# Two heads' values as high and low halves of one stationary operand in a dilated attention layer

## The chip, the cores and the metric

The kernel runs on one core of one Trainium2 chip. The metric is the device time of one execution in microseconds (us); the number shown is the median over runs.

## What is computed

Two layers on 512 tokens of width 1024, in fp32. Layer 0 mixes by stick-breaking attention, layer 1 by the dilated attention that this change touches; each is followed by a feed-forward block and a gate. The dilated attention has three groups with dilation 1, 4 and 16, eight heads of width 64 in each. A group's attention is banded and gives, beside its output, the logarithm of the sum of its weights; the groups are then mixed by a softmax over these logarithms. That equals one softmax over the keys of all three groups together, which is what the kernel computes.

```python
for g, (window, dil) in enumerate(((128, 1), (512, 4), (2048, 16))):
    q = apply_partial_rope(proj[:, :, g, 0], cos, sin)
    k = apply_partial_rope(proj[:, :, g, 1], cos, sin)
    v = proj[:, :, g, 2]
    ...
    o, lse = banded_attention(strided(q), strided(k), strided(v), window // dil)
    ...
alpha = jax.nn.softmax(jnp.stack(lses, axis=0), axis=0)
o = jnp.einsum('gbsh,gbshd->bshd', alpha, jnp.stack(outs, axis=0).astype(jnp.float32)).astype(x.dtype)
return o.reshape(B, S, H * HEAD_DIM) @ w_out
```

## The kernel before

Every fp32 product is made of high and low parts in the fp32r type by three matmuls: high x high, low x high, high x low (`mm3`, L257 to L259; `linear`, L356 to L360; `value_step`, L667 to L669). Weights arrive in 220 units of 128x1024 by SP's transfers; ACT makes the high part (L98), DVE the low part (L99).

TensorE (PE) runs in program order. `Filler` puts pieces of the projections (queries, keys, values, output products) between the attention's steps by a clock that the steps advance. The order on ACT, DVE, GpSimd (POOL) and SP comes from a scheduler that simulates the program with priorities (`due`, the table `TUNE`). PSUM has two banks for projections (`bank`, shown as mmb and out) and six others (`wide`, shown as wb).

`dilated` (L640 to 945) works in this order. The values of groups 1 and 2 for the first four heads are projected into four wide banks, those of group 0 for all heads into two of each kind; `value_part` empties them, high part by ACT (L680), low part by DVE (L681), 128 columns (two heads) at a time. `sq.row` in between spreads the norm's factors over a bank with fp32 calls (L311) and DVE copies them to `rrow` (L320). Then for each of four pairs of heads: `scores` (matmuls L731, mask and maximum by DVE L741), `maxima` over the three groups (transposes L749 to L763, steps on `m` L755 to L757), and `exps`, 16 exponentials on ACT (L778). Group 0 is in natural order of the tokens (order 0); groups 1 and 2 share a second order (order 1), in which a token 4r + c stands at c x 128 + r; `cut` and `sigma` are the two views.

`attend` runs after the maxima of pairs 0 and 1 for one pair, and at the end for pairs 2 and 3 together, with the rest of the values and the first output products between (`between`; the exponentials of the last pair that are in `late` wait for the last values). A pair has eight jobs (head, order, half of the tokens). `turn` transposes a job's weights (L794), and ACT and DVE make the high and low part (`th` L800, `tl` L801). `apply` multiplies them with the values. It runs `ahead` (3) jobs behind `turn`. The stationary operand is 128 columns wide, 64 of them values and 64 ones (zeros in the low part), so that the sums of the weights come out in the other half of the bank:

```python
vs, vp = slice(64 * h, 64 * h + P), pr % 2 if g else pr
mm3(out[:, j * P:j * P + width], v[:, 0, vp, vs], v[:, 1, vp, vs],
    th[:, at:at + width], tl[:, at:at + width], j == 0 and g < 2, True)
```

After each head the two orders' banks are added (ACT L856, DVE L858); after each pair `divide` takes four reciprocals of `den` (L833), one after each following job, then the product (L835) and the split into `od` (L262, L264), with which `out` multiplies the output weights.

Of the kernel before, what the change touches and what calls it, by code (L numbers as in the profile page):

```python
# [29 lines left out]
            hps=2, blag=1.5, vlag=0.0, fx=5.5, ahead=3, pgap=0.0, vev1=50)  # L30
# [4 lines left out]
C_ID, C_NEG, C_TRI, C_M0, C_M1, C_M2, C_ROPE, C_END = 0, 128, 256, 384, 640, 768, 896, 898  # L35

# [6 lines left out]
def constants():  # L43
    i = np.arange(P)
    c = np.zeros((P, C_END), np.float32)
    c[:, C_ID:C_ID + P] = np.eye(P)
    c[:, C_NEG:C_NEG + P] = np.where(i[:, None] >= i[None, :], -BIG, 0.0)
# [116 lines left out]
def program(tc, ctx, w_dram, x_dram, xs_dram, p_dram, pos_dram, g_dram, c_dram, out_dram):  # L164
# [33 lines left out]
    nc.sync.dma_start(consts, c_dram)  # L198
# [441 lines left out]
    def dilated(xh, xl, sq, oh, ol, partial, out, prepare):  # L640
        swap = list(range(8, 16)) + list(range(8)) + list(range(16, 32))
        with tc.tile_pool(name="dlw", bufs=1, reuse_waits="tile") as wp:
            V, norm, qk, whole = {}, {}, {}, []
# [6 lines left out]
            def ones_and_zeros():  # L650

                for v in whole:
                    n = v.shape[3]
                    pool.tensor_copy(v[:, :, 0, :, 64:128], ones[:, 0:1, None, None].to_broadcast([P, 4, n, 64]))
                    pool.tensor_scalar(v[:, :, 1, :, 64:128], ones[:, 0:1, None, None].to_broadcast([P, 4, n, 64]),
                                       0.0, None, ALU.mult)
# [14 lines left out]
            def value_part(g, t, ps):  # L671
                v = V[g, t]
# [97 lines left out]
            def exps(S, N):  # L770
                done = []
                for h in range(2):
                    for order in range(2):
                        for i in range(4):
                            s = S[h, order, i // 2]
                            a, b = (i % 2) * 256 + (P if (i == 0 and order == 0) else 0), (i % 2 + 1) * 256
                            with due("exps"):
                                done.append(act.activation(s[:, a:b], s[:, a:b], AF.Exp, bias=N[:, order, i, h:h + 1],  # L778
                                                           scale=0.125))
                return done  # L780

            def turn(S, order, h, j2):
# [3 lines left out]
                for j in (2 * j2, 2 * j2 + 1):  # L786
# [10 lines left out]
                th = wp.tile([P, T], F32R, name="th", tag="th", bufs=3)  # L797
                tl = wp.tile([P, T], F32R, name="tl", tag="tl", bufs=3)
# [4 lines left out]

            def apply(pr, order, h, j2, th, tl, out):
                at = 0
                for j in (2 * j2, 2 * j2 + 1):
# [4 lines left out]
                    for g, width in jobs:  # L811
                        v = V[g, j]
                        vs, vp = slice(64 * h, 64 * h + P), pr % 2 if g else pr
                        mm3(out[:, j * P:j * P + width], v[:, 0, vp, vs], v[:, 1, vp, vs],
                            th[:, at:at + width], tl[:, at:at + width], j == 0 and g < 2, True)
                        at += width
                fill.clock += 1.3

            def attend(prs, gap, between=None):
                jobs = [(pr, order, h, j2) for pr in prs for h in range(2) for order in range(2) for j2 in range(2)]  # L820
                outs, sums = {}, {}
# [8 lines left out]
                def divide(pr, num, den):  # L830
                    for c in range(4):
                        cs = slice(c * P, (c + 1) * P)
                        i = dve.reciprocal(den[:, cs], den[:, cs])  # L833
                        if c == 3:
                            dve.tensor_mul(num, num, den)  # L835
# [26 lines left out]
                for d in list(later):  # L862
                    run(d)
# [333 lines left out]
```

## Time and profile before

| | |
|---|---|
| median of three runs | 1458.36 us (1457.98, 1461.53, 1458.36) |
| the profiled execution | 1462.61 us |
| its span | 1460.5 us, mean granted clock 0.984 |
| PE busy | 1419.4 us, 97% |
| DVE busy | 910.5 us, 62% |
| ACT busy | 639.8 us, 44% |
| the dilated attention | about 714 to 1030 us of the span |

A row of a group of instructions has line, engine, operation, what is written and read (partitions x elements, type) and how many, then busy us, mean ns of one, and idle time just before them with what ended it. A timeline's row starts with start and length. Matmuls are pipelined: their listed lengths overlap, so what one costs PE is the distance from its start to the next. An fp32 call to the matmul stands as two records.

### The profile page before, as it was taken

The numbers are of one execution on the slowest core, as the hardware profiler recorded it, in microseconds if no ns is written. First come the engines' busy times: TensorE is split into PE (matmuls) and PEld (weight loads), VectorE is DVE, ScalarE is ACT, GpSimd is POOL, SyncE is SP. The second block draws the span as 40 slices with busy tenths as digits, with TensorE's granted clock in tenths as the row PEclk, the third lists the DMA queues.
The fourth block names the chain that finished last, engine by engine and source line by source line (L and its number), as shares of the span: only waits on it lengthen the run. The fifth ranks groups of instructions, "written<-read, shape, count | busy, mean of one in ns | idle before, by whom it ended". The sixth has DMA issues, their size and how long they took to land.

```text
span 1460.5 us, 18457 instructions
## 1 busy us (share of the span) xinstructions
PE 1419.4 (97%) x7250; PEld 1194.4 (82%) x7250; DVE 910.5 (62%) x1539; ACT 639.8 (44%) x970; POOL 56.9 (4%) x33
## 2 busy tenths in 40 slices
PE   8999999999999999999989999999999999999998
PEld 7888988888888888887868878788888888888877
DVE  4788886584353544568758886956783443535476
ACT  4788985543231222345542433444732322312353
POOL 0111110000000000001200000000000000000000
PEclk9999999999999999999999998999999999999999
DMA  5344351433333333223322211220432332333321
GB/s 201 101 115 119 111 134 58 137 95 101 100 89 100 94 94 101 87 85 117 109 72 88 73 57 45 73 74 14 145 101 89 100 101 87 101 92 96 101 76 70
DMA packets 45127, 138.80 MB, mean 95 GB/s; under 512 B 5680, under 2 KB 6448, under 8 KB 45040
## 3 DMA queue, kind: packets, MB, share of 16 engines
q1 hardware_dynamic: 44960, 137.36, 31.2%
q8 instruction: 57, 0.93, 0.3%
q0 software_dynamic: 80, 0.26, 0.1%
q14 instruction: 30, 0.25, 0.0%
HBM read 123.45 MB, written 4.19 MB: 87 GB/s over the span
## 4 chain that ended last, share of the span: by engine, by line
PE 87%; DVE 8%; ACT 2%; issue 1%; DMA 1%; SPq 0%; ACTq 0%; DVEq 0%
PE wb L356 17%; PE wb L358 16%; PE wb L360 16%; PE mmb L356 5%; PE mmb L360 5%; PE mmb L358 5%; DVE wlo L99 2%; PE wb L258 1%; PE wb L259 1%; PE wb L257 1%; PE mmb L419 1%; PE mmb L421 1%; PE mmb L420 1%; PE wb L731 1%; PE z L259 1%
## 5 line engine op out<-in xcount | busy, mean ns | idle before, releaser
L98 ACT ACTIVATE whi<-wraw_t 128x1024 fp32r<-128x1024 f32 (+1 forms) x298 | 229.2, 800 | 468.3 <-PE wb L360 345.7
L99 DVE TENSOR_TENSOR wlo<-wraw_t,whi 128x1024 fp32r<-128x1024 f32 (+1 forms) x310 | 276.2, 912 | 238.8 <-ACT whi L98 233.7
L356 PE MATMUL wb<-nh,whi 128*128 128x512 f32 (+1 forms) x594 | 227.1, 385 | 4.3 <-ACT nh L262 4.3
L358 PE MATMUL wb<-nh,wlo 128*128 128x512 f32 (+1 forms) x594 | 226.1, 383 | 0.0
L360 PE MATMUL wb<-nl,whi 128*128 128x512 f32 x576 | 207.4, 390 | 0.4 <-DVE nl L266 0.4
L356 PE MATMUL wb<-fh,whi 128*128 128x512 f32 x496 | 196.2, 396 | 0.0
L358 PE MATMUL wb<-fh,wlo 128*128 128x512 f32 x496 | 196.2, 396 | 0.0
L360 PE MATMUL wb<-fl,whi 128*128 128x512 f32 x496 | 196.2, 396 | 0.0
L356 PEld LDWEIGHTS wb<-nh,whi 128*128 128x128 f32 x594 | 111.6, 188 | 28.8 <-ACT nh L262 6.9
L358 PEld LDWEIGHTS wb<-nh,wlo 128*128 128x128 f32 x594 | 111.6, 188 | 21.8
L360 PEld LDWEIGHTS wb<-nl,whi 128*128 128x128 f32 x576 | 107.7, 188 | 23.4 <-DVE nl L266 1.2
L356 PEld LDWEIGHTS wb<-fh,whi 128*128 128x128 f32 x496 | 93.2, 188 | 22.6
L360 PEld LDWEIGHTS wb<-fl,whi 128*128 128x128 f32 x496 | 93.2, 188 | 22.5
L358 PEld LDWEIGHTS wb<-fh,wlo 128*128 128x128 f32 x496 | 93.2, 188 | 22.5
L356 PE MATMUL mmb<-nh,whi 128*128 128x512 f32 x248 | 102.2, 412 | 3.6 <-DVE V L681 3.6
L360 PE MATMUL mmb<-nl,whi 128*128 128x512 f32 x248 | 98.9, 399 | 0.0
L358 PE MATMUL mmb<-nh,wlo 128*128 128x512 f32 x248 | 98.9, 399 | 0.0
L1087 DVE TENSOR_TENSOR f<-wb,f 128x512 f32<-128x512 f32 (+1 forms) x50 | 33.3, 667 | 73.6 <-PE wb L360 71.2
L1062 DVE TENSOR_TENSOR z<-wb,rrow 128x512 f32<-128x512 f32 x60 | 40.6, 688 | 55.7 <-PE wb L360 55.7
L1065 ACT ACTIVATE fh<-z 128x512 fp32r<-128x512 f32 x64 | 39.9, 632 | 77.1 <-DVE z L1063 77.0
L356 PEld LDWEIGHTS mmb<-nh,whi 128*128 128x128 f32 x248 | 48.1, 194 | 13.6 <-issue 4.0
L289 DVE TENSOR_TENSOR acc<-acc,sq 128x512 f32<-128x512 f32 (+1 forms) x74 | 48.9, 661 | 15.6 <-ACT sq L285 15.0
(817 smaller groups left out, 2665.3 us busy)
## 6 DMA issues: line engine op xcount, KB each, us to landing
wraw_t<-w SPq DMA_DIRECT2D x219, 512.0 KB, 3.6
x<-x SPq DMA_DIRECT2D x8, 256.0 KB, 6.9
h<-xs SPq DMA_DIRECT2D x8, 256.0 KB, 5.6
spill<-h SPq DMA_DIRECT2D x8, 256.0 KB, 2.7
h<-spill SPq DMA_DIRECT2D x8, 256.0 KB, 5.5
out<-h SPq DMA_DIRECT2D x7, 256.0 KB, 2.1
praw<-p SPq DMA_DIRECT2D x4, 256.0 KB, 4.0
wraw_t<-w SPq DMA_DIRECT2D x4, 128.0 KB, 3.1
```

What stands on the lines that cost most here:

```text
L98: self.highs.append(self.nc.scalar.activation(hi[:, c], src[:, c], AF.Copy))
L99: self.lows.append(self.nc.vector.tensor_sub(lo[:, c], src[:, c], hi[:, c].bitcast(F32)))
L257: pe.matmul(ps, ah, bh, start=start, stop=False, skip_group_check=True)
L258: pe.matmul(ps, ah, bl, start=False, stop=False, skip_group_check=True)
L259: pe.matmul(ps, al, bh, start=False, stop=stop, skip_group_check=True)
L289: self.adder.tensor_tensor(self.acc[:, cs], self.acc[:, cs], self.sq[:, cs], ALU.add)
L356: pe.matmul(ps[m][:, cs], wh, xh[k][:, cs], start=(k == 0 and cs is not TWO[1]), stop=False, skip_group_check=True)
L358: pe.matmul(ps[m][:, cs], wl, xh[k][:, cs], start=False, stop=False, skip_group_check=True)
L360: pe.matmul(ps[m], wh, xl[k], start=False, stop=(k == nk - 1), skip_group_check=True)
L1062: dve.tensor_mul(z, ps, norm["row"])
L1065: act.activation(a, z, AF.Copy)
L1087: dve.tensor_add(y[m][:, cs], ps, y[m][:, cs])
```

## The change

The tile of values holds for each head its high and low part side by side, so one stationary operand of 128 columns is high | low, and a job is multiplied by two matmuls (th, tl) instead of three. Its bank then has th x high + tl x high in 64 rows and th x low + tl x low in the other 64, which are added afterwards (L874 and L875 of the new file). The sums of the weights come from the exponentials' own accumulators, `D`; ACT widens them to 64 columns for each head (`wD`), and eight fp32 calls for each pair (L844, L847) spread them over a bank that the reciprocals read. Both orders go to one bank, `av`: order 0 is transposed with a permuted identity (`sorter`) and written in runs of 32 columns (`mixed`). `ahead` is 4, the buffers of th and tl are 5. `value_part` is one instruction on each engine for a bank's part.

```diff
-                v = wp.tile([P, 4, 2, 2 if g else 4, 192], F32R, name=f"V{g}")
-                whole.append(v)
+                v = wp.tile([P, 4, 4 if g else 8, 2, 64], F32R, name=f"V{g}")
...
-                for pr in range(2 if g else 4):
-                    at = (t % 2 if g else 0) * 256 + pr * P
-                    src = ps[:, at:at + P].rearrange("p (h d) -> p h d", h=2)
-                    hi, lo = (v[:, i, pr, :].rearrange("p (h d) -> p h d", h=3)[:, 0:3:2] for i in range(2))
-                    with due("vev1"):
-                        norm["last"] = act.activation(hi, src, AF.Copy, scale=c)
-                        dve.scalar_tensor_tensor(lo, src, c, hi.bitcast(F32), ALU.mult, ALU.subtract)
+                at = (t % 2 if g else 0) * 256
+                src = ps[:, at:at + (256 if g else 512)].rearrange("p (h d) -> p h d", d=64)
+                hi, lo = (V[g, t][:, :, i] for i in range(2))
+                with due("vev1"):
+                    norm["last"] = act.activation(hi, src, AF.Copy, scale=c)
+                    dve.scalar_tensor_tensor(lo, src, c, hi.bitcast(F32), ALU.mult, ALU.subtract)
...
                                 done.append(act.activation(s[:, a:b], s[:, a:b], AF.Exp, bias=N[:, order, i, h:h + 1],
-                                                           scale=0.125))
-                return done
+                                                           scale=0.125, accum_out=D[:, order, i, h:h + 1]))
+                wD = wp.tile([P, 2, 4, 2, 64], F32, name="wD")
+                with due("exps"):
+                    act.activation(wD, D[:, :, :, :, None].to_broadcast([P, 2, 4, 2, 64]), AF.Copy)
+                return done, wD
...
-                        pe.transpose(ps[:, n:n + P], part, ident)
+                        pe.transpose(ps[:, n:n + P], part, ident if order else sorter)
...
+            def mixed(ap, a, n):
+
+                return ap.rearrange("p (r c m) -> p c r m", r=4, c=4)[:, a // P:(a + n) // P]
+
...
-                        mm3(out[:, j * P:j * P + width], v[:, 0, vp, vs], v[:, 1, vp, vs],
-                            th[:, at:at + width], tl[:, at:at + width], j == 0 and g < 2, True)
+                        v = V[g, j][:, (pr % 2 if g else pr) * 2 + h].rearrange("p a d -> p (a d)")
+                        dst = out[:, j * P:(j + 1) * P] if order else mixed(out, j * P, width)
+                        for t in (th, tl):
+                            src = t[:, at:at + width]
+                            pe.matmul(dst, v, src if order else src.rearrange("p (c r m) -> p c r m", r=4, m=32),
+                                      start=(j == 0 and order == 0 and t is th), stop=(order == 1 and t is tl),
+                                      skip_group_check=True)
...
-                fill.clock += 1.3
+                fill.clock += 0.9
...
+                    ps = wide()
+                    for order in (1, 0):
+                        for i in range(4):
+                            d = DD[pr][:, order, i].rearrange("p a d -> p (a d)")
+                            if order:
+                                pe.matmul(ps[:, i * P:(i + 1) * P], d, ident, start=(i == 0), stop=False,
+                                          skip_group_check=True)
+                            else:
+                                pe.matmul(mixed(ps, i * P, P), d, sorter.rearrange("p (c r m) -> p c r m", r=4, m=32),
+                                          start=False, stop=True, skip_group_check=True)
+                    fill.clock += 1.8
                     for c in range(4):
                         cs = slice(c * P, (c + 1) * P)
-                        i = dve.reciprocal(den[:, cs], den[:, cs])
...
+                        yield dve.reciprocal(den[:, cs], ps[:, cs])
...
-                            act.activation(s1, outs[1], AF.Copy)
-                            for dst, src in ((den[hs], ds), (num[hs], hs)):
-                                dve.tensor_tensor(cut(dst), sigma(outs[0][src]), cut(s1[src]), ALU.add)
+                            act.activation(num[hs], av[ls], AF.Copy)
+                            dve.tensor_tensor(num[hs], av[hs], num[hs], ALU.add)
                         if h == 1:
-                            later.append(divide(pr, num, den))
+                            dve.tensor_mul(num, num, den)
+                            oh[pr], ol[pr] = split(num, f"od{pr}")
```

Not shown: the permuted identity is a part of the constants' input, which one more transfer of SP brings; `ones_and_zeros` (six POOL instructions that filled the ones and zeros) is gone; a pair's `divide` starts with the pair's first job, one piece after each job, and `attend` no longer runs what is left of it behind its loop.

The order on DVE, behind the copy to `natural` in the norm before the dilated layer (`V` are the low parts of values, `ang`, `turns`, `angle` and `mag` steps of the rope's angles, `wlo` a weight's low part). Before:

```order
L297 COPY natural<-acc 128x4x128
L305 TENSOR_SCALAR ms<-mmb 128x8
L99 TENSOR_TENSOR wlo<-wraw_t,whi 128x1024
L681 SCALAR_TENSOR_TENSOR V_5870<-wb,rcol,V_5870 128x2x64
L681 SCALAR_TENSOR_TENSOR V_5871<-wb,rcol,V_5871 128x2x64
L681 SCALAR_TENSOR_TENSOR V_5870<-wb,rcol,V_5870 128x2x64
L618 CAST ang<-pos_i 128x512
L681 SCALAR_TENSOR_TENSOR V_5871<-wb,rcol,V_5871 128x2x64
L681 SCALAR_TENSOR_TENSOR V_5870<-wb,rcol,V_5870 128x2x64
L681 SCALAR_TENSOR_TENSOR V_5871<-wb,rcol,V_5871 128x2x64
L619 TENSOR_SCALAR ang<-ang,consts 128x512
L681 SCALAR_TENSOR_TENSOR V_5870<-wb,rcol,V_5870 128x2x64
L320 COPY rrow<-mmb 128x512
```

and in the change, from its angle's fifth step on:

```order
L628 SCALAR_TENSOR_TENSOR angle<-turns,ang 128x512
L629 SCALAR_TENSOR_TENSOR angle<-turns,angle 128x512
L675 SCALAR_TENSOR_TENSOR V_5871<-wb,rcol,V_5871 128x4x64
L630 SCALAR_TENSOR_TENSOR angle<-turns,angle 128x512
L675 SCALAR_TENSOR_TENSOR V_5871<-wb,rcol,V_5871 128x4x64
L675 SCALAR_TENSOR_TENSOR V_5872<-wb,rcol,V_5872 128x4x64
L632 TENSOR_SCALAR angle<-angle 128x512
L675 SCALAR_TENSOR_TENSOR V_5871<-wb,rcol,V_5871 128x4x64
L322 COPY rrow<-mmb 128x512
L634 TENSOR_SCALAR mag<-angle 128x512
L101 TENSOR_TENSOR wlo<-wraw_t,whi 128x1024
```

Seven pieces of values of 128 columns and the weight's low part stood ahead of `rrow`; now four of 256 do, and the weight's low part is behind it.

The order on ACT, at the exponentials of the third pair (`kh` and `qh` are the high parts of a split, `whi` a weight's). Before:

```order
L778 ACTIVATE S<-S,negmax 128x128
L778 ACTIVATE S<-S,negmax 128x256
L98 ACTIVATE whi<-wraw_t 128x1024
L778 ACTIVATE S<-S,negmax 128x256 x8
L778 ACTIVATE S<-S,negmax 128x128
L262 ACTIVATE qh<-rf_8021 128x512
L778 ACTIVATE S<-S,negmax 128x256 x5
L98 ACTIVATE whi<-wraw_t 128x1024
L262 ACTIVATE kh<-rf_8086 128x512
```

and in the change:

```order
L774 ACTIVATE S,D<-S,negmax 128x128
L774 ACTIVATE S,D<-S,negmax 128x256 x9
L774 ACTIVATE S,D<-S,negmax 128x128
L264 ACTIVATE kh<-rf_7978 128x512
L774 ACTIVATE S,D<-S,negmax 128x256 x3
L100 ACTIVATE whi<-wraw_t 128x1024
L774 ACTIVATE S,D<-S,negmax 128x256 x2
L778 ACTIVATE wD<-D 128x1024
```

The split of k stood behind all 16 exponentials and a weight's split, and now stands behind 11 exponentials; the copy to `wD` follows the sixteenth.

The order on PE, at the start of the last attend (`S` are weights, `out` the first output products). Before:

```order
L794 MATMUL wb<-consts,S 128x128 x11
L257 MATMUL wb<-th,V_5869 128x256
L258 MATMUL wb<-tl,V_5869 128x256
L259 MATMUL wb<-th,V_5869 128x256
```

and in the change:

```order
L793 MATMUL wb<-consts,S 128x128 x15
L820 MATMUL wb<-th,V_5870 128x2x4x32
L820 MATMUL wb<-tl,V_5870 128x2x4x32
L820 MATMUL wb<-th,V_5870 128x2x4x32
L820 MATMUL wb<-tl,V_5870 128x2x4x32
L793 MATMUL wb<-consts,S 128x128 x4
L844 MATMUL wb<-consts,wD 128x128 x4
L847 MATMUL wb<-consts,wD 128x4x32 x4
L259 MATMUL out<-od0h,whi 128x512
```

Four more transposes stand ahead of the first apply, two matmuls take the place of three, and the sums' calls follow the next transposes.

## Rows read from the trace of the kernel before

**Rows 1.** The page's first part: busy us, share of the span, instructions.
```profile
PE 1419.4 (97%) x7250; PEld 1194.4 (82%) x7250; DVE 910.5 (62%) x1539; ACT 639.8 (44%) x970; POOL 56.9 (4%) x33
```

**Rows 2.** Waits of PE, 700 to 1030: us in total, times, longest.
```profile
PE mmb L667 <- DVE rrow L320: 3.8, 1, 3.8
PE mmb L356 <- DVE V L681: 3.6, 1, 3.6
PE wb L763 <- DVE m L757: 1.9, 1, 1.9
PE out L257 <- DVE V L681: 1.9, 1, 1.9
...
PE wb L731 <- ACT kh L262: 1.1, 1, 1.1
...
PE wb L731 <- DVE kl L264: 0.9, 1, 0.9
PE wb L763 <- DVE m L756: 0.7, 1, 0.7
```

**Rows 3.** Windows: length, busy us (instructions) by engine, PE clock, DMA share, GB/s.
```profile
734.00:738.00 4.00, 4.00 (x12) 3.13 (x11) 3.97 (x13) 1.35 (x5) 0.00 (x0) 0.57 0.02 4
872.00:878.00 6.00, 6.00 (x18) 4.78 (x19) 2.79 (x5) 3.82 (x10) 0.00 (x0) 0.51 0.30 87
946.00:953.00 7.00, 6.82 (x30) 5.83 (x31) 4.91 (x34) 0.63 (x1) 0.00 (x0) 0.51 0.23 77
990.00:994.00 4.00, 4.00 (x17) 3.48 (x16) 0.07 (x1) 3.90 (x10) 0.00 (x0) 0.57 0.00 0
```

**Rows 4.** Groups by form, PE, 700 to 1030: busy us, mean ns | idle before.
```profile
L259 PE MATMUL wb<-th,V 128*128 128x128 f32 x72 | 20.1, 279 | 0.0
...
L259 PE MATMUL wb<-th,V 128*128 128x256 f32 x24 | 7.0, 294 | 0.0
```

**Rows 5.** Timeline of PE in three places: start, us, engine, line, operation.
```profile
727.99 1.05 PE L311 MATMUL mmb<-consts,rcol 128*128 128x128 f32 x8
728.80 0.48 PE L667 MATMUL mmb<-whi,uh 128*128 128x512 f32 x1
...
978.81 0.28 PE L667 MATMUL mmb<-whi,nh 128*128 128x256 f32 x1
...
981.93 0.28 PE L669 MATMUL mmb<-wlo,nh 128*128 128x256 f32 x1
...
994.27 0.27 PE L259 MATMUL wb<-th,V 128*128 128x128 f32 x1
...
995.28 0.28 PE L259 MATMUL wb<-th,V 128*128 128x128 f32 x1
```

**Rows 6.** Timeline of DVE at 732.
```profile
732.85 0.69 DVE L320 COPY rrow<-mmb 128x512 f32<-128x512 f32 x1
```

**Rows 7.** Timeline of ACT and PE at 754 to 760.
```profile
754.56 0.37 ACT L680 ACTIVATE V<-mmb,rcol 128x128 fp32r<-128x128 f32 x1 [2.52 <-PE mmb L669]
...
760.19 0.47 PE L356 MATMUL mmb<-nh,whi 128*128 128x512 f32 x1 [3.63 <-DVE V L681]
```

**Rows 8.** Groups by form, DVE, 700 to 1030.
```profile
L801 DVE TENSOR_TENSOR tl<-wb,th 128x512 fp32r<-128x512 f32 x24 | 16.0, 678 | 10.6 <-ACT th L800 10.4
...
L833 DVE RECIPROCAL den<-den 128x128 f32<-128x128 f32 x16 | 13.9, 917 | 0.0
...
L741 DVE DVE_READ_ACCUMULATOR2_ANT M<- 128x1 f32 x96 | 7.9, 82 | 0.0
```

**Rows 9.** Timeline of PE, two groups of transposes four jobs apart.
```profile
997.04 0.62 PE L794 MATMUL wb<-consts,S 128*128 128x128 f32 x4
...
1002.84 0.62 PE L794 MATMUL wb<-consts,S 128*128 128x128 f32 x4
```

**Rows 10.** Timeline of PE at 55, and the answer on line 481 (two runs of 128).
```profile
54.99 0.33 PE L483 MATMUL z<-sb0qa,sb0la 128*128 128x256 f32 x1
...
L481 PE MATMUL z<-rconst x16: 328/328/332, 55.2 to 225.8; 128*128 128x256 f32 x16
```

More of the change, by code (lines that the diff above doesn't have):

```diff
@@ L29 @@
             fb=0.32, slope=0.05, lag=8.0, gap=1.2, m0=6.0, m1=5.5, m2=8.0, p0=5.0, p1=2.0, p2=8.0, hp0=6, hp1=30,
-            hps=2, blag=1.5, vlag=0.0, fx=5.5, ahead=3, pgap=0.0, vev1=50)
+            hps=2, blag=1.5, vlag=0.0, fx=5.5, ahead=4, pgap=0.0, vev1=50)
 NUNIT = 220
@@ L44, in constants @@
     i = np.arange(P)
-    c = np.zeros((P, C_END), np.float32)
+    c = np.zeros((P, C_ALL), np.float32)
     c[:, C_ID:C_ID + P] = np.eye(P)
+    c[:, C_SORT:C_SORT + P] = np.eye(P)[:, i.reshape(32, 4).T.reshape(-1)]
     c[:, C_NEG:C_NEG + P] = np.where(i[:, None] >= i[None, :], -BIG, 0.0)
@@ L771, in exps @@
                 done = []
+                D = wp.tile([P, 2, 4, 2], F32, name="D")
                 for h in range(2):
@@ L828, in attend, with divide @@
                     between()
-                def divide(pr, num, den):
+                def divide(pr, den):
+                    ps = wide()
[9 more added lines that the diff above has]
+                    fill.clock += 1.8
                     for c in range(4):
                         cs = slice(c * P, (c + 1) * P)
-                        i = dve.reciprocal(den[:, cs], den[:, cs])
-                        if c == 3:
-                            dve.tensor_mul(num, num, den)
-                            oh[pr], ol[pr] = split(num, f"od{pr}")
-                            later.clear()
-                        yield i
-                for n, (pr, order, h, j2) in enumerate(jobs):
-                    if j2 == 0:
-                        outs[order] = wide()
-                    apply(pr, order, h, j2, *ready.pop(0), outs[order])
+                        yield dve.reciprocal(den[:, cs], ps[:, cs])
+                for n, (pr, order, h, j2) in enumerate(jobs):
+                    if order == 0 and j2 == 0:
+                        if h == 0:
+                            sums[pr] = tmp("num"), tmp("den")
+                            later.append(divide(pr, sums[pr][1]))
+                        av = wide()
+                    apply(pr, order, h, j2, *ready.pop(0), av)
                     if n + ahead < len(jobs):
@@ L847, in attend @@
                     if later:
-                        after(next(later[0]), norm["turned"])
+                        i = next(later[0], None)
+                        if i is None:
+                            later.clear()
+                        else:
+                            after(i, norm["turned"])
                     if order == 1 and j2 == 1:
-                        if h == 0:
-                            sums[pr] = tmp("num"), tmp("den")
                         num, den = sums[pr]
-                        s1 = tmp("s1")
-                        hs, ds = HALF[h], HALF[1 - h]
+                        hs, ls = HALF[h], HALF[1 - h]
                         with due("comb"):
-                            act.activation(s1, outs[1], AF.Copy)
-                            for dst, src in ((den[hs], ds), (num[hs], hs)):
-                                dve.tensor_tensor(cut(dst), sigma(outs[0][src]), cut(s1[src]), ALU.add)
+                            act.activation(num[hs], av[ls], AF.Copy)
+                            dve.tensor_tensor(num[hs], av[hs], num[hs], ALU.add)
                         if h == 1:
-                            later.append(divide(pr, num, den))
+                            dve.tensor_mul(num, num, den)
+                            oh[pr], ol[pr] = split(num, f"od{pr}")
                     tick(gap)
-                for d in list(later):
-                    run(d)
             vps = {g: [wide(), wide()] for g in (1, 2)}
@@ L924, in dilated @@
                 N = maxima(MM[pr])
-                late = exps(SS[pr], N)[TUNE["late"]:]
+                late, DD[pr] = exps(SS[pr], N)
+                late = late[TUNE["late"]:]
                 fill(TUNE["m2"])
```

27 lines of the change are left out of this document (10 added, 17 removed).

## The prediction

> **What bounds the kernel now.** I read the page's busy times first. TensorE (PE) is busy for 97% of the span, VectorE (DVE) for 62%, ScalarE (ACT) for 44% [rows 1]. So a matmul that goes is worth its own time, and work on the other engines is worth only what PE waits for. Then I read the waits of PE over the dilated attention, 700 to 1030 us [rows 2]: all seven that stand there, 13.9 us together, are of kinds that the change touches. Third, the windows in which the granted clock fell: 0.51 to 0.57 in the stretches just behind those waits, the lower of the two levels for most of the stretch [rows 3]. A wait can therefore cost more than its own length, and I take the loss behind it as (1 - clock) times the stretch: 1.7 us behind 734, 2.9 behind 872, 3.4 behind 946, 1.7 behind 990.
>
> The sum is made against the profiled execution of 1462.61 us (span 1460.5). The median of the runs, 1458.36, lies 4.25 lower; I subtract the sum's gain from the median, as the runs will be.
>
> **Matmuls removed and added.** The third matmul of every product with the weights goes: 72 of 128 columns and 24 of 256 [rows 4]. What one costs is its distance to the next, not its listed duration, for they are pipelined: from 994.27 to 995.28 there are nine steps, 0.112 each; from 978.81 to 981.93 26 steps, 0.120 each [rows 5]. 72 x 0.112 + 24 x 0.120 = 10.9 us. Added are 32 fp32 calls that spread the sums (8 for each pair of heads). The kernel has such calls already, in the row that spreads a column: four calls are eight records, 727.99 to 728.80, 0.101 each [rows 5]. 64 x 0.101 = 6.5 us. Net gain 4.4 us; with the added ones at 0.112, 3.7.
>
> By the Trainium skill ("TensorE: Matmul & The Clock Gate", Back-to-back issue gap) a sustained stream of 128-column matmuls runs at about 81 ns each. Taken for both kinds, that page would make the net (96 - 64) x 0.081 = 2.6 us, an estimate; the rows here show 0.112, and I keep them.
>
> **The rrow wait, 3.8 us.** PE needs a bank that DVE empties with the copy to rrow, at 732.85 for 0.69 [rows 6]. Ahead of it in DVE's order stood a weight split, seven pieces of values and two steps of the angle. In the new order four pieces of 256 and eight steps of the angle are ahead, and the split is behind. Those pieces can go as their banks fill, and the angle's steps between them, while PE still works on the last ones; the copy's own source is written by the calls from 727.99 to 728.80 [rows 5]. So the copy should start about 729 and end about 729.8. PE asked at 732.85 + 0.69 - 3.84 = 729.7, but one late piece is 0.5, so I keep 0.7 as the wait: gain 3.1. The low clock behind it (1.7) I count half, 0.9, because a short wait stays. Bounds 0 and 5.5.
>
> **The wait for group 0's values, 3.6 us.** Values of the first group are emptied in 32 pieces of 128 that pass between ACT and DVE with weight splits in between; the first starts at 754.56, yet PE gets its bank at 760.19, 3.63 after it asked [rows 7]. Now it is one ACT and one DVE instruction of 512 for each bank. By the 512-wide th and tl of this kernel (DVE's is 678 ns [rows 8]) a bank is empty about 1.3 us after its last matmul, 754.56 + 1.3 = 755.9, before PE asks at 756.56. Gain 3.6, with 0 as the lower bound if weight splits stand between them as they did before.
>
> **The waits at the maxima, 1.9 + 0.7 us.** Pair 1's maxima wait for two DVE steps on m. Ahead of them stood four reciprocals in one go and a sum that are now elsewhere or gone: 4 x 0.87 (13.9 us for 16) and one step of 512 at tl's 0.68, 4.2 us less on DVE [rows 8], more than both waits. Gain 2.6, and half of the low clock behind them, 1.4, since other work of DVE's could still come late. Bounds 0 and 5.5.
>
> **The waits for kh and kl, 1.1 + 0.9 us.** ACT split k only after all 16 exponentials of the pair and a weight split; now it stands after 11. That is five exponentials and one split earlier, but the accumulators add to each exponential, by the nearest row up to 82 ns, DVE's read of its accumulator [rows 8]: 11 x 0.08 = 0.9 back. And DVE's kl has its own queue. I take half: 1.0, and a quarter of the low clock, 0.9. Bounds -1 and 5.4.
>
> **The wait for an out bank, 1.9 us.** It ends with the last of the second half's values, which ACT and DVE hand to and fro in 128-wide pieces. Half the instructions are left. Gain 1.9, and half of the low clock, 0.9. Bounds 0 and 3.6.
>
> **What the last attend may cost.** Here PE has nothing to fill with but a few output products. A pair is eight jobs, twice the four between 997.04 and 1002.84 [rows 9], 11.6 us. Now it takes 11.6 - (18 x 0.112 + 6 x 0.120) + 16 x 0.101 = 10.5. DVE's share of a pair: six tl of 512 columns at 0.68 and two of 384 at three quarters of it, 5.1; four reciprocals, 3.5; two adds, the product and the split of num at 0.68 each, 2.7 [rows 8]: 11.3, less where neighbours overlap. The two are about level, and the last pair's reciprocals, which stood behind the loop, are now in it. So PE may wait on tl in each pair. I charge 2.0 of waits and one low stretch of 1.6, 3.6 in all; bounds 0 and 8. Five th and tl buffers and one more turn ahead work against it: the first apply now follows 15 transposes, not 11, so its th has more time.
>
> **Covered.** The four 1024-wide copies of the sums (at most 1.4 us each, twice tl's 0.68) and the accumulators' reads (64 x 0 to 82 ns, at most 5.2 us [rows 8]) lie on ACT, 44% busy; in the last attend they delay th by up to 2 us, which is inside the bound of 8. The half-size num steps, the ones and zeros gone from GpSimd and the extra transfer of 64 KB at SP's head, next to loads that run at the start, are off PE's path. If ACT's cover were gone the accumulators would cost those 5.2.
>
> **Sum.** 4.4 + (3.1 + 0.9) + 3.6 + (2.6 + 1.4) + (1.0 + 0.9) + (1.9 + 0.9) - 3.6 = 17.1 us. Against the profiled 1462.6 that is 1445.5; against the median **1441.3**. With the terms at their likely spread its own range is 1435 to 1448.
>
> **Rivals.**
> *Only the count moves.* The waits that go come back elsewhere, since ACT and DVE still do nearly the same work and PE asks sooner. For it: each wait is one late step among several. Against it: they hang on four different queues. Then 1458.4 - 4.4 = 1454.0, just at 0.3% below.
> *The last attend is paced by DVE.* With PE idle a little in every job the granted clock stays low over part of the stage; a third of two pairs' 21 us at half speed is 7 more, 1448.3. The Trainium skill ("TensorE: Matmul & The Clock Gate", A second HAM failure mode: psum-queue depth-cycling) tells of a kernel whose short idles between groups made the clock swing; the stretches of [rows 3] agree that it falls behind waits, here of 0.9 us and more.
> *Everything goes.* No charge in the last attend and all of the low clock: 17.1 + 3.6 + 5.6 = 26.3, 1432.1.
> *Slower: matmuls that write in runs of 32 columns.* The outputs of order 0 and the spread sums of order 0 now land in the bank as runs of 32, 64 + 32 = 96 records. The nearest row, a matmul of 256 columns that writes two runs of 128, lists 328 ns, where contiguous ones of 256 list 280 [rows 5, 10]: 0.05 for one break. Per break that is 7 breaks on 48 matmuls, 3 on 16 and on 32: 16.8 + 2.4 + 4.8 = 24 us, 1465.3. It passes the gain from 17.1 / 96 = 0.18 us a record. Against it: a contiguous 256-wide one just before lists 0.33 too [rows 10], so the row may show no price of a break at all. The Trainium skill ("PSUM — Partial Sum Buffer", Specifications (TRN2)) says that any non-contiguous pattern slows matmuls significantly; no row here shows it for runs of 32.
>
> **How the numbers follow.** Forecast 0.56; only the count 0.18; DVE-paced 0.12; everything 0.07; slower 0.07. About 0.3%, 4.4 us, is what a measurement of this kernel can tell from no change. Half of the second case lies within it, the last case above: faster 0.84, same 0.09, slower 0.07. The range 1431 to 1456 leaves out the slower case and about a tenth from the edges of the others.
>
> **What would show it.** Right: 192 matmuls of the new apply at 0.111 and 0.120 distance, whatever their listed duration; 64 records of the spread at about 0.10; no PE wait over 1 us for rrow, values at 760, m or an out bank; clock near 1.00 behind them. Wrong: distances of 0.2 and more at the writes in runs; PE waits on tl or on reciprocals between jobs with the clock under 0.9 from 982 to 1015; ACT rows for the accumulators long enough that th is late. The sum is wrong if waits of the same length stand at other lines.

## The result, and the profile after

The changed kernel takes 1431.45 us (median of 4 runs, 1430.79 to 1431.52), the kernel before on the same chip 1459.47. The ratio is 0.9816, 95% interval 0.9801 to 0.9831: 28.0 us less. The forecast was 1441.3 in a range of 1431 to 1456. The sign and the range hold, the range by half a microsecond; the size does not: 17 us were forecast, 28 came. The rival in which nothing is charged for the last attend and all of the low clock goes stood at 1432.1.

The page's first part of the changed kernel, to be read against [rows 1]:

```profile
PE 1401.6 (98%) x7218; PEld 1181.3 (83%) x7218; DVE 899.3 (63%) x1503; ACT 643.4 (45%) x1010; POOL 46.1 (3%) x27
```

PE is busy 17.8 us less, ACT 3.6 us more. How far the 28 us are waits, clock or matmuls is read from one window that goes from the layer's first matmul of values to the last output product into the bank `out`. The view of windows (length, then busy us of PE, weight load, DVE, ACT, GpSimd with instructions, PE clock, DMA share, GB/s) of the kernel before:

```profile
697.20:1027.40 330.20, 308.91 (x1902) 267.21 (x1901) 243.55 (x560) 140.98 (x256) 9.64 (x6) 0.94 0.23 69
```

and of the changed kernel:

```profile
696.00:996.10 300.10, 291.77 (x1870) 253.39 (x1870) 232.62 (x524) 145.19 (x296) 2.58 (x2) 0.98 0.26 81
```

The stretch is 30.1 us shorter, 330.2 to 300.1. PE's idle time in it went from 330.2 - 308.9 = 21.3 to 300.1 - 291.8 = 8.3: **13.0 us of waits**. Its busy time fell by 17.1. Of that the matmuls are 10.9 - 6.5 = **4.4** by the forecast's distances, which the rows of the changed kernel below bear out; what is left, **12.7**, is put down to the clock, whose mean in the window rose from 0.94 to 0.98 (0.06 x 330 = 20 us lost before, 0.02 x 300 = 6 after).

PE's waits in the changed kernel, in the form of [rows 2], all over 0.5 us:

```profile
PE wb L793 <- ACT S L774: 2.4, 2, 1.3
PE wb L725 <- DVE kl L266: 1.9, 1, 1.9
PE wb L820 <- DVE tl L800: 1.3, 2, 1.0
PE mmb L303 <- DVE natural L299: 1.3, 1, 1.3
```

Those for `rrow`, for the values, for both steps on `m`, for `kh` and for an out bank are gone. kl is there again, at another pair, and one is new: transposes that wait for exponentials (S L774).

The places in the timeline of PE that answer to [rows 6, 7]. At `rrow`, the matmul before and the one that needs the bank:

```profile
727.46 0.40 PE L664 MATMUL mmb<-wlo,uh 128*128 128x512 f32 x1
727.94 0.50 PE L662 MATMUL mmb<-whi,uh 128*128 128x512 f32 x1
```

0.48 between two starts, about 0.25 of idling where it was 3.84. At the last value of group 0 and the first query:

```profile
748.95 0.39 PE L664 MATMUL wb<-wlo,uh 128*128 128x512 f32 x1
749.17 0.39 PE L358 MATMUL mmb<-nh,whi 128*128 128x512 f32 x1
```

No wait at all where it was 3.63.

Groups by form, against [rows 4, 8]:

```profile
L820 PE MATMUL wb<-tl,V 128*128 128x128 f32 x72 | 17.7, 280 | 0.3 <-DVE tl L800 0.3
...
L774 ACT ACTIVATION_READ_ACCUMULATOR S<-S,negmax 128x1 f32 x64 | 12.3, 192 | 0.0
...
L820 PE MATMUL wb<-tl,V 128*128 128x256 f32 x24 | 6.4, 285 | 1.0 <-DVE tl L800 1.0
...
L844 PE MATMUL wb<-consts,wD 128*128 128x128 f32 x32 | 4.2, 276 | 0.0
```

The new apply's matmuls with tl list 280 and 285 ns, like those of before; the spreading calls 276. What they cost is the distance of their starts. In the last attend, two 256-wide applies of order 0 and the sums' calls, L847 in runs of 32 columns, up to the next matmul:

```profile
962.95 0.28 PE L820 MATMUL wb<-th,V 128*128 128x256 f32 x1
963.07 0.28 PE L820 MATMUL wb<-tl,V 128*128 128x256 f32 x1
...
963.63 1.06 PE L844 MATMUL wb<-consts,wD 128*128 128x128 f32 x8
964.52 1.06 PE L847 MATMUL wb<-consts,wD 128*128 128x128 f32 x8
965.33 0.48 PE L259 MATMUL out<-od0h,whi 128*128 128x512 f32 x1
```

0.12 for an apply; eight records take 0.89 and 0.81, 0.111 and 0.101 each, so the 64 cost 6.5 to 7.1 us. The row of L774 is one that the kernel before did not have: ACT's read of an accumulator, 192 ns each, 12.3 us.

The last attend, from its first transposes to the last of its reciprocals, in the view of windows:

```profile
959.00:988.00 29.00, 27.42 (x217) 25.83 (x216) 22.53 (x34) 20.50 (x51) 0.00 (x0) 1.00 0.35 110
```

The clock is 1.00 and PE idles 1.6 of 29 us. Behind the kl wait the clock still falls, as the window shows (0.43 x 4 = 1.7 us lost):

```profile
843.19 0.33 PE L725 MATMUL wb<-kl,qh 64*128 64x128 f32 x2 [1.92 <-DVE kl L266]
```

```profile
845.00:849.00 4.00, 4.00 (x17) 3.42 (x17) 2.63 (x19) 0.00 (x0) 0.00 (x0) 0.57 0.45 131
```

### The profile page after: what moved, and what is told of

Its sections match the earlier page's. It is cut to its first block, busy times and chain, and to the rows that moved or that the text cites. A ratio compares the mean times of both kernels' runs of the same rounds, so it can differ in the third digit from the quotient of the medians.

```text
span 1429.3 us, 18374 instructions
## 1 busy us (share of the span) xinstructions
PE 1401.6 (98%) x7218; PEld 1181.3 (83%) x7218; DVE 899.3 (63%) x1503; ACT 643.4 (45%) x1010; POOL 46.1 (3%) x27
## 4 chain that ended last, share of the span: by engine, by line
PE 87%; DVE 7%; ACT 4%; issue 1%; DMA 1%; SPq 0%; ACTq 0%; DVEq 0%
PE wb L358 17%; PE wb L360 17%; PE wb L362 17%; PE mmb L358 5%; PE mmb L362 5%; PE mmb L360 5%; ACT S L774 1%; DVE wlo L101 1%; PE mmb L421 1%; PE mmb L422 1%; PE mmb L423 1%; PE wb L725 1%; PE z L261 1%; PE z L259 1%; PE z L260 1%
## 5 line engine op out<-in xcount | busy, mean ns | idle before, releaser
L291 DVE TENSOR_TENSOR acc<-acc,sq 128x512 f32<-128x512 f32 (+1 forms) x74 | 48.8, 659 | 15.6 <-ACT sq L287 15.0
L362 PEld LDWEIGHTS mmb<-nl,whi 128*128 128x128 f32 x248 | 46.9, 189 | 10.2
```

The lines of the kernel that those rows point to most:

```text
L291: self.adder.tensor_tensor(self.acc[:, cs], self.acc[:, cs], self.sq[:, cs], ALU.add)
L362: pe.matmul(ps[m], wh, xl[k], start=False, stop=(k == nk - 1), skip_group_check=True)
```

## The experiments

Three theories stood against each other. A: the gain is PE's waits and the low clock behind them, beside a few us of count, and each wait has its own part of the change. B: fewer columns and deeper lookahead give the gain. C: the clock falls in those places whether PE waits or not. "Above the changed kernel" is counted from the 1431.45 of the result; that kernel was not run again beside the experiments, and the medians of the kernel before, which was, lie between 1458.28 and 1460.89. So differences under about 3 us are not clear as times, and there the traces have to speak.

**Values in narrow pieces again (narrow_values).**

```diff
-                at = (t % 2 if g else 0) * 256
-                src = ps[:, at:at + (256 if g else 512)].rearrange("p (h d) -> p h d", d=64)
-                hi, lo = (V[g, t][:, :, i] for i in range(2))
+                for pr in range(2 if g else 4):
+                    at = (t % 2 if g else 0) * 256 + pr * P
+                    src = ps[:, at:at + P].rearrange("p (h d) -> p h d", d=64)
+                    hi, lo = (V[g, t][:, 2 * pr:2 * pr + 2, i] for i in range(2))
...
```

> The changed kernel with the values emptied in pieces of 128 columns again, everything else as changed. Theory A (most of the gain is PE's waits and the low clock behind them, and the wide evacuation took away the waits for rrow, for group 0's values and for an out bank): PE waits of 3 to 8 us come back at those three places, the clock falls behind them, and the time is 7 to 12 us above the changed kernel (1438 to 1443). Theory B (fewer columns, two matmuls instead of three and a deeper lookahead give the gain; the evacuation is covered by PE's work): within 2 us of the changed kernel.

Measured: 1439.42 (ratio to before 0.987, 0.985 to 0.9889), 8.0 above the changed kernel. Its waits of PE for values:

```profile
PE mmb L358 <- DVE V L676: 3.6, 1, 3.6
...
PE out L259 <- DVE V L676: 0.5, 1, 0.5
```

and its timeline of PE behind the first:

```profile
750.23 0.47 PE L358 MATMUL mmb<-nh,whi 128*128 128x512 f32 x1 [3.63 <-DVE V L676]
...
750.81 0.63 PE L362 MATMUL mmb<-nl,whi 128*128 128x512 f32 x1
751.23 0.63 PE L358 MATMUL mmb<-nh,whi 128*128 128x512 f32 x1
```

The wait for group 0's values came back with its full 3.6, and the clock fell behind it: the matmuls at 750.81 and 751.23 stand 0.42 apart. The out bank came back with 0.5 only, `rrow` not at all. So the wide evacuation is the cause at one of the three places, a part of it at the second, and not at `rrow`. The wait was 3.6 before and is 3.6 here, but before, the clock behind it was 1.00: the same wait costs more here.

**rrow ahead of the values, in the kernel before (rrow_first).**

```diff
-                dve.tensor_copy(r, ps)
+                self.copied = dve.tensor_copy(r, ps)
...
-                        dve.scalar_tensor_tensor(lo, src, c, hi.bitcast(F32), ALU.mult, ALU.subtract)
+                        low = dve.scalar_tensor_tensor(lo, src, c, hi.bitcast(F32), ALU.mult, ALU.subtract)
+                        if g and "rope" not in norm:
+                            after(low, sq.copied)
```

> The kernel before with one thing changed: DVE copies rrow ahead of the low parts of the values of groups 1 and 2. Theory A: the wait of 3.84 us for rrow shrinks to under 1 us and the clock stays at its upper level behind it, 1.7 us more; 4 to 6 us under the kernel before, if the pieces that now come later hold nobody up. Theory C (the clock falls at this place whether PE waits or not): 2 to 4 us under it, and the clock is still low after 734. Theory B: 0 to 2 us, because the values' pieces come later and another wait takes its place.

Measured: 1452.81 (10 runs, 1448.46 to 1456.64) against 1458.28 (13 runs), ratio 0.9958, 0.9941 to 0.9974: 5.5 less. The wait in the timeline of PE, and the window behind it:

```profile
731.54 0.49 PE L667 MATMUL mmb<-whi,uh 128*128 128x512 f32 x1 [2.62 <-DVE rrow L320]
```

```profile
734.00:738.00 4.00, 4.00 (x19) 3.33 (x18) 4.00 (x13) 3.00 (x8) 0.00 (x0) 1.00 0.00 0
```

The wait shrank only from 3.84 to 2.62, yet the clock behind it is 1.00, where it was 0.57 [rows 3]. That speaks against C at this place. It does not show that 1.2 us less idling ended the stretch, for in the same trace a stretch stands where the kernel before had 1.00, behind the wait of 3.6 for group 0's values, which did not change:

```profile
757.00:763.00 6.00, 6.00 (x21) 4.75 (x20) 1.06 (x4) 0.69 (x3) 0.00 (x0) 0.72 0.13 52
```

The one behind the maxima lost less (0.28 x 6 = 1.7 us from 870 to 876, where it was 2.9), and from 985 to 1020 the clock is 1.00, though the waits there for tl and for an out bank stayed (1.7 in all, and 1.3 where it was 1.9). So the 5.5 us are not the price of the `rrow` wait alone. On DVE a weight's split and the angle's steps still stand ahead of the copy:

```profile
728.34 1.23 DVE L99 TENSOR_TENSOR wlo<-wraw_t,whi 128x1024 fp32r<-128x1024 f32 x1 [5.81 <-ACT whi L98]
...
730.80 0.68 DVE L320 COPY rrow<-mmb 128x512 f32<-128x512 f32 x1
```

**rrow held up in the changed kernel (rrow_held_5).**

```diff
-                dve.tensor_copy(r, ps)
+                for _ in range(again + 1):
+                    dve.tensor_copy(r, ps)
...
-                    row = sq.row()
+                    row = sq.row(again=5)
```

> The changed kernel with the copy to rrow done six times in a row on DVE instead of once (five of 0.69 us added, the same result). Theory A: PE waits about 3.5 us more at this place, and the clock falls behind it as it did before the change, 1.7 us more: 4.5 to 6 us above the changed kernel. Theory C (the low clock is not caused by such waits): 3 to 3.7 us above it with a clock of 1.00 behind the wait. Theory B: less than 2 us, because DVE has room.

Measured: 1442.46, 11.0 above the changed kernel, more than forecast. The five copies did not run in a row: the scheduler put values and angle steps between them. The timeline of PE and the window behind:

```profile
734.67 0.77 PE L663 MATMUL mmb<-whi,uh 128*128 128x512 f32 x1 [7.18 <-DVE rrow L323]
```

```profile
734.00:740.00 6.00, 5.33 (x14) 4.25 (x15) 1.82 (x3) 0.00 (x0) 0.00 (x0) 0.57 0.01 3
```

6.9 more of wait and a clock of 0.57 in 6 us (2.6 lost) are 9.5 of the 11.0; the stretch behind the kl wait is longer too, 0.57 from 851 to 859. A holds in kind, and this is the edit that shows a wait bringing a low stretch to a place that had none; the size of the wait was off.

**A third matmul of zeros in the changed kernel (third_matmul).**

```diff
-                        for t in (th, tl):
+                        for s, t in ((v, th), (none, th), (v, tl)):
...
-                            pe.matmul(dst, v, src if order else src.rearrange("p (c r m) -> p c r m", r=4, m=32),
+                            pe.matmul(dst, s, src if order else src.rearrange("p (c r m) -> p c r m", r=4, m=32),
```

> The changed kernel with a third matmul in every product of weights and values, whose stationary operand is zeros (96 matmuls, 72 of 128 columns and 24 of 256; it adds nothing to the result). Theory A and B on the count: 72 x 0.112 + 24 x 0.120 = 10.9 us above the changed kernel if PE has no idle time there, 9 to 11 with the 3 to 4 us of waits in the attends partly filled. If the matmuls removed had lain beside waits in the attends anyway: under 5 us.

Measured: 1436.93, only 5.5 above. The wait for tl that is left in its attends and the window behind the place where kl was waited for:

```profile
PE wb L822 <- DVE tl L802: 0.9, 1, 0.9
```

```profile
844.00:850.00 6.00, 6.00 (x44) 5.38 (x43) 5.79 (x23) 0.59 (x1) 0.00 (x0) 1.00 0.29 87
```

The wait for kl is gone, 1.9, and the low stretch behind it too; tl has 0.9 in place of 1.3. The added matmuls lay in part where PE would have waited. 10.9 - 1.9 - 0.4, less the 1.7 of low clock behind kl in the changed kernel, leaves 6.9; the spans, 1435.8 and 1429.3, show 6.5.

**The kernel before with two matmuls (before_two).** It leaves out the low part of the values.

```diff
-                        mm3(out[:, j * P:j * P + width], v[:, 0, vp, vs], v[:, 1, vp, vs],
-                            th[:, at:at + width], tl[:, at:at + width], j == 0 and g < 2, True)
+                        for t in (th, tl):
+                            pe.matmul(out[:, j * P:j * P + width], v[:, 0, vp, vs], t[:, at:at + width],
+                                      start=(j == 0 and g < 2 and t is th), stop=(t is tl), skip_group_check=True)
```

> The kernel before without the third matmul of the products with the weights: it leaves out the low part of the values. 96 matmuls, 10.9 us, go and nothing comes. Theory A (count, waits and clock are separate terms): 10.9 less some 2 to 5 us of new waits in the attends, 6 to 9 us under the kernel before, and the waits for rrow, group 0's values and an out bank stay. Rival (fewer matmuls alone also end the low stretches behind 860): more than 13 us under it.

Measured: 1455.87 (10 runs) against 1459.32 (12 runs), ratio 0.9974, 0.9963 to 0.9985: 3.5 less, of 10.9 us of matmuls that went. Three of its waits of PE, and the windows of the last attend, of the kernel before and of this one:

```profile
PE wb L815 <- DVE tl L801: 4.0, 4, 2.0
PE mmb L667 <- DVE rrow L320: 3.8, 1, 3.8
PE mmb L356 <- DVE V L681: 3.6, 1, 3.6
```

```profile
982.00:1020.00 38.00, 33.78 (x235) 30.89 (x235) 24.84 (x39) 19.32 (x42) 0.00 (x0) 0.91 0.09 28
976.00:1014.00 38.00, 31.98 (x194) 28.37 (x194) 26.31 (x43) 19.69 (x42) 0.00 (x0) 0.82 0.25 84
```

The waits of before stay, that for the out bank at 1.4 instead of 1.9; tl is waited for 4.0 instead of 1.7, and the clock of the last attend is 0.82 where it was 0.91: 0.09 x 38 = 3.4 us more lost, a part of it while PE idled. Here only the count moves: alone, it gives a third of itself.

**Reciprocals in one go behind the pair (late_divide).**

```diff
                         if h == 0:
                             sums[pr] = tmp("num"), tmp("den")
-                            later.append(divide(pr, sums[pr][1]))
...
                         if h == 1:
+                            run(divide(pr, den))
                             dve.tensor_mul(num, num, den)
```

> The changed kernel with a pair's eight spreading calls and four reciprocals in one go behind the pair's last job, as the reciprocals stood before, instead of one piece after each of its first jobs. Theory A (the waits at pair 1's maxima, 1.9 and 0.7, went because the reciprocals no longer stand ahead of the steps on m): one or both come back, with low clock behind them, 2 to 6 us above the changed kernel; the product and split of the last pair come later too. Theory B (they went because DVE has 0.7 us of the sum less and the lookahead is deeper): within 1.5 us.

Measured: 1432.72, 1.3 above. Its waits of PE for `m`, and the window behind them:

```profile
PE wb L757 <- DVE m L751: 2.5, 1, 2.5
...
PE wb L757 <- DVE m L750: 1.0, 1, 1.0
```

```profile
916.00:924.00 8.00, 7.36 (x22) 5.97 (x23) 3.11 (x6) 6.19 (x25) 0.00 (x0) 0.57 0.22 66
```

Both waits came back, at another pair's maxima, with a low stretch behind them. That points to their cause: the reciprocals end at 902.2 in DVE's queue, and DVE works without a gap from there to the steps on `m` at 912.57 and 915.89. It costs little in sum, since the kl wait and its low stretch went in exchange.

**Three jobs of lookahead (ahead_3).** `ahead` 4 to 3, buffers of th and tl 5 to 3.

> The changed kernel with three jobs of lookahead and three buffers of th and tl, as before the change, instead of four and five. Theory A: PE waits 1 to 4 us more for th and tl in the attends, most in the last one, and the clock may fall there (982 to 1015 under 0.97): 1 to 6 us above the changed kernel. Rival (lookahead plays no part): within 1 us.

Measured: 1434.06 (0.9827, 0.9807 to 0.9846), 2.6 above.

```profile
PE wb L793 <- ACT S L774: 4.5, 2, 3.3
```

```profile
874.00:880.00 6.00, 6.00 (x50) 5.01 (x49) 4.78 (x19) 2.31 (x4) 0.00 (x0) 0.72 0.30 90
```

Not where it was expected: the last attend keeps a clock of 1.00, but the first jobs of an attend wait longer for exponentials, 4.5 in place of 2.4, with a low stretch behind the longer one (0.28 x 6 = 1.7 us), while kl's wait is gone.

**The four parts undone together (parts_undone):** narrow values, the third matmul (with the clock's step of 1.3 as before), late reciprocals, three jobs of lookahead.

> The changed kernel with four parts undone at once: values emptied in pieces of 128, a third matmul of zeros, the reciprocals in one go behind the pair, three jobs of lookahead with three buffers. The accumulators, the one output bank and the runs of 32 columns stay. Theory A (these four carry the gain, and each costs the low clock behind its wait): 1450 to 1460, near the kernel before, with waits at the values, the maxima and an out bank. Rival (the gain lies in the one output bank, or in an order that these do not touch): under 1447.

Measured: 1447.02 (0.9914, 0.9894 to 0.9935), 15.6 above the changed kernel; the single parts add up to 8.0 + 5.5 + 1.3 + 2.6 = 17.4. Two of its waits at places that the change touched, and the clock behind the first stretch:

```profile
PE mmb L358 <- DVE V L678: 3.6, 1, 3.6
...
PE out L259 <- DVE V L678: 1.4, 1, 1.4
```

```profile
760.00:1010.00 250.00, 242.88 (x1622) 210.09 (x1621) 194.13 (x466) 113.50 (x255) 0.00 (x0) 1.00 0.21 63
```

Theory A's range is missed, and 1447.02 stands at the edge of the rival's: the four carry 15.6 of the 28 us, and 10.9 of these are the third matmul by count. What they do not bring back is the clock: it is 1.00 from 760 to 1010, and one stretch stands behind group 0's values. `rrow` is waited for 0.3, both steps on `m`, kh and kl not at all. So what ended the low stretches behind 860 lies in what was not undone, the one output bank, the sums from the accumulators, the weight's split behind `rrow` or the order that the scheduler made of them; which of these was not tried. Since rrow_first lost stretches at places that its edit did not touch, it may also be no more than the new timing of the waits.

**Three edits that change nothing, or little.**

ones_back, the six GpSimd instructions put back on a spare tile:

> The changed kernel with the six GpSimd instructions that filled ones and zeros put back, writing a spare tile that nobody reads. Theory A2 (they were not off the path, as the prediction had it: they held up the positions' transfer and the norm's column rcol on GpSimd, so that DVE's work ahead of rrow came late): PE waits 2 us or more at rrow or at the values' banks behind it, and the time is 2 to 6 us above the changed kernel. Theory A1 (they are covered, as the prediction had it, and the rrow wait went by the order of the weight's split alone): within 1 us.

1430.42, the same as the changed kernel. They were covered.

contiguous, with outputs of order 0 in one run, which leaves them in another order of tokens (`dst = out[:, j * P:j * P + width]`, and the spreading calls likewise):

> The changed kernel with the 96 records that write in runs of 32 columns writing in one run each (order 0 then stands in another order in the bank, so heads' outputs are mixed up among tokens). Theory A: within 1 us of the changed kernel, runs of 32 cost nothing, since the records of the new apply stand 0.11 and 0.12 apart. Rival (the slower case of the prediction): 5 to 24 us under the changed kernel.

1430.78, the same. Runs of 32 columns cost nothing here.

no_sums, without `accum_out` and with `wD` made on GpSimd:

> The changed kernel without the accumulators of the exponentials and with the widened copy made by GpSimd from other values: it leaves out the sums of the weights, so the division is by something else. It takes 64 reads of 0.19 us and four copies of 1.05 us off ACT, 16.5 us. Theory A: PE's two waits for exponentials at the start of the first two attends (1.25 and 1.16) go, the rest was covered: 1 to 4 us under the changed kernel. Rival (ACT's extra work holds up the splits of q and k and the high parts as well): 5 to 10 us under it.

1429.04, 2.4 less; it leaves out the sums that the reciprocals need. The waits for exponentials are gone from its list; kl stays:

```profile
PE wb L725 <- DVE kl L266: 1.9, 1, 1.9
```

**Larger distances of the filling (lag_m2):** `m2` and `lag` 8 to 10.

> The changed kernel with two distances of the filling raised from 8 to 10: between a pair's exponentials and its attend, and between a projection's last step and the scores that use it. Theory A: the waits that are left there (kl 1.9, exponentials 1.25 and 1.16) and the low clock behind kl go without others coming: 3 to 6 us under the changed kernel (1425 to 1428.5). Theory B (waits come back elsewhere, since the filling that moved is missing in the attends): within 2 us either way.

1432.29, no gain. kl is gone, but

```profile
PE wb L743 <- DVE M L740: 2.4, 1, 2.4
PE wb L793 <- DVE M L735: 1.5, 1, 1.5
```

2.4 and 1.5 us of waits for the masked scores came in its place. No run with the whole computation in it was clearly under the changed kernel.

## Why the prediction was right, and where its size was off

**Right in kind.** The waits went at the places named. The sum came out 11 us short, though. That the time lies inside the range is luck: it lies 0.45 us above the lower bound, and the runs of the changed kernel alone differ by 0.7. What came is close to the rival to which the forecast gave 0.07. Summed over the seven kinds of [rows 2], 13.9 us became 1.9; the forecast took 12.2. The new wait for exponentials takes 2.4 back, so 3.4 of the 13.0 went at places that the forecast did not name, the waits for tl (2.6 to 1.3) and for the norm's `acc` (1.6 to 0.5) the largest. Group 0's values: 3.6 forecast, 3.6 measured, and narrow_values gives it back. The maxima: 2.6 forecast and measured, and late_divide brings such waits back, at another pair, by the cause given. `rrow`: 0.7 was left in the forecast, 0.25 is; no experiment shows which part of the change took it, the split of a weight that now stands behind the copy or the fewer pieces. The out bank: all of it went, though narrow_values brings only 0.5 back, so the wide pieces are not its whole cause. The runs of 32 columns and the GpSimd instructions cost nothing, as forecast, and the extra transfer shows no cost: the dilated layer starts at 696.0, not later than before (697.2). The page of the Trainium skill on PSUM ("PSUM — Partial Sum Buffer", Specifications (TRN2)) has any non-contiguous pattern slow matmuls significantly. The run contiguous does not show it for runs of 32 columns: 1430.78 without them, 1431.45 with them.

**The count.** 4.4 net holds by the distances to within half a microsecond: new matmuls at 0.11 and 0.12, half of the spreading calls at 0.101 and half at 0.111, 0.3 us more than the forecast's 6.5. The experiments correct how a count is used: 10.9 us of matmuls were worth 5.5 in the changed kernel and 3.5 in the kernel before, since matmuls also cover what PE would wait for. That a matmul that goes is worth its own time, as the forecast put it, is what they contradict.

**The step that failed: the low clock behind the waits.** The forecast counted halves and a quarter, 0.9 + 1.4 + 0.9 + 0.9 = 4.1, and charged 1.6 for a new low stretch: 2.5 net. Measured were 12.7. Every low stretch of [rows 3] went, and a new one of 1.7 us stands behind the kl wait. Two that the forecast did not count went as well; the view of windows of the kernel before has them, and the stretch behind the wait at 760. The first row is a stretch behind the norm's waits that the changed kernel has too, in the second block:

```profile
720.00:728.00 8.00, 6.93 (x35) 6.84 (x35) 1.35 (x3) 2.25 (x3) 1.67 (x1) 0.57 0.35 98
760.00:766.00 6.00, 5.81 (x26) 4.85 (x27) 1.78 (x9) 1.22 (x5) 0.00 (x0) 1.00 0.22 78
891.00:897.00 6.00, 5.33 (x23) 4.51 (x24) 4.96 (x28) 0.60 (x1) 0.00 (x0) 0.54 0.30 89
1014.00:1018.00 4.00, 4.00 (x16) 3.38 (x16) 2.89 (x4) 1.20 (x2) 0.00 (x0) 0.57 0.00 0
```

```profile
719.00:727.00 8.00, 7.83 (x41) 7.84 (x42) 5.76 (x14) 4.68 (x8) 1.83 (x1) 0.57 0.22 66
```

0.46 x 6 and 0.43 x 4 are 4.5 us more that were lost there. With the forecast's 9.7 and less the new 1.7 that is 12.5, the 12.7 within what such windows tell. Halving was wrong because the loss does not shrink with the wait: a shorter wait for `rrow` in rrow_first has no stretch behind it, an unchanged wait for group 0's values has one there and none in the kernel before, and the stretch behind the maxima went from 2.9 to 1.7. Every low stretch in these windows stands behind waits of PE, and rrow_held_5 shows that a wait can bring one; which part of the change ended those behind 860 is not shown, for parts_undone does not bring them back.

**The second step that failed: the charge for the last attend, 3.6.** It is about 0: clock 1.00, 1.6 us idle, 1.3 of it at the first apply. before_two shows that the fear was right for the old structure, with 4.0 us for tl and a clock of 0.82 where it was 0.91, as soon as the third matmul is missing. It is not the lookahead that saved it, for ahead_3 keeps 1.00 there. What else differs is that a pair has two adds on DVE, not four, that both orders share a bank, and that the spreading calls give PE 16 more records in each pair, which before_two does not have; which of these decides was not tried alone.

**kh and kl.** Forecast 1.0 and 0.9 of clock. kh's 1.1 and kl's 0.9 went, and a kl wait of 1.9 with a low stretch came at another pair: about nothing net in waits. The accumulators' bound was too low: 82 ns were taken from DVE, ACT's read takes 192, and the first attends wait 2.4 us for exponentials. no_sums prices that at 2.4, a difference that is not clear as a time.

By its own sum: waits 12.2 - 2.0 forecast, 13.0 measured; count 4.4 and 4.4; clock 2.5 and 12.7. The profiled execution of before lay 4.25 above the median of its runs, so some of the 30.1 us are that execution's own; the medians show 28.0. Its clock was 0.984, where the runs of before at 1458.3 to 1458.9 have 0.988, so that surplus most likely belongs to the clock term.

## What to carry to other kernels

When PE is near 100% busy, read the granted clock behind each wait before counting instructions: behind waits of 0.7 to 4 us stood low stretches that cost 1.7 to 3.4 us each, or none, and the length of the wait did not tell which. Removing matmuls alone turns in part into waits and low clock; it is worth looking for the work that stands ahead of a late step in another engine's queue. Undo parts one at a time and all at once: here four parts explain 16 of 28 us, and the end of the low stretches behind 860 is not tied to any one part.

## What the runs showed that was not expected

An accumulator's read on ACT takes 192 ns after each exponential of about 0.5 us. A matmul that writes runs of 32 columns is as fast as one that writes in one run (1430.78 against 1431.45). Not every wait was followed by a low clock: 3.6 us at 760 in the kernel before was followed by 1.00 (the window 760 to 766 above), the same wait in narrow_values by distances of 0.42. Which of them is followed by one stays open. The kernels with many waits also spread more from run to run, 1455.3 to 1462.8 in 13 runs of the kernel before against 1430.8 to 1431.5 in 4 of the changed one; the granted clock goes with it, 0.991 in the run of 1455.3 and 0.984 in that of 1462.8. What makes it differ from run to run stays open.
